# Two hybrid decoder layers: separate PSUM banks for even and odd blocks of a norm, later column sums, mLSTM heads ahead of MoBA, and the residual behind the convolutions

## The chip, the core and the metric

One core of a Trainium2 chip runs the whole program. TensorE (PE) does the matrix products, VectorE (DVE), ScalarE (ACT) and GpSimd (POOL) work on tiles of 128 partitions in the on-chip memory, and SyncE (SP) issues the loads from HBM. Products land in PSUM, eight banks of 128 x 512 float32, which DVE and ACT read. The metric is the device time of one execution in microseconds; the median of the runs counts.

## What is computed

A trunk of two layers on 256 tokens of width 1024, all in float32. Each layer has three sublayers, each with a modulation from a conditioning vector and a layer norm behind it:

```
def reference(x, c, ...):
    for l in range(DEPTH):
        mod = (silu(c) @ ada_w[l] + ada_b[l]).reshape(b_, 3, 3, D_MODEL)
        y = swiglu(modulate(x, mod[:, 0, 0], mod[:, 0, 1]), ffn_w13[l, 0], ffn_w2[l, 0])
        x = layer_norm(ALPHA * x + 0.5 * (1 + mod[:, 0, 2]) * y, ln_g[l, 0], ln_b[l, 0])
        y = token_mixer(modulate(x, mod[:, 1, 0], mod[:, 1, 1]), w_in[l], w_out[l], ...)
        x = layer_norm(ALPHA * x + (1 + mod[:, 1, 2]) * y, ln_g[l, 1], ln_b[l, 1])
        y = swiglu(modulate(x, mod[:, 2, 0], mod[:, 2, 1]), ffn_w13[l, 1], ffn_w2[l, 1])
        x = layer_norm(ALPHA * x + 0.5 * (1 + mod[:, 2, 2]) * y, ln_g[l, 2], ln_b[l, 2])
```

The token mixer projects the input once (`w_in`) and gives the columns to three groups of heads of width 64: six heads of a gated delta rule (GDN) over chunks of 64 tokens, with a causal convolution and SiLU ahead; four heads of MoBA, which for 256 tokens is causal softmax attention; six mLSTM heads, also with a convolution ahead, whose output is multiplied with a sigmoid of a gate projection, normed per head and scaled. The three outputs stand side by side (`mix`) and go through `w_out`.

## The kernel before

The program has six phases in a row, FFN, mixer, FFN for each layer, with a boundary (layer norm, modulation, start of the next phase) between any two.

**Products.** Each float32 weight comes by DMA into a tile `raw` and is split: ACT copies it to a rounded `hi` (L101), DVE subtracts to `lo` (L104). Each product is three matmuls (`mm3`, L109 to L111), with hi and lo of both sides. The splits run all through the kernel, so ACT and DVE have weight splits between whatever else they do.

**Order.** SP's order is that of the code. For PE, DVE and ACT a scheduler sorts the instructions of each phase; inside a boundary, from the norm to the first lines of the next phase, the order is that of the code too. `tc.issue_after` holds an instruction behind another.

**Boundary.** `Norm` reads the finished PSUM rows in two token halves t = 0, 1: `gate` multiplies with the gate row (L320), `add` adds the residual `xa` (L325), `square` and `stats` make the statistics, `scale` normalises (L354). `turn(t, q)` transposes four 128 x 128 blocks k of a half into one PSUM bank (L440); `mod` applies scale and shift per block into `xm`, even k on ACT (L450), odd k on DVE (L448); `high` (L454) and `low` (L459) split the outcome into `xh` and `xl`, which the first product of the next phase takes (`nx["product"]`). Some of the adaptation columns are summed here (`late`, L225, matmuls of one column with `ones`).

**Adaptation.** `ada_block` computes one of nine blocks of `silu(c) @ ada_w` in four background items (`bg`) within the FFN phases: DVE accumulates `adacc` from loads `araw` (L260). `fin` then sums over partitions on PE, as columns (L225) or, for a gate block, as broadcast rows (L233). For blocks in `late` the boundary calls `fin`; for all others the fourth item does.

**Mixer.** `gt` and `zs` are copied from the first product. `gdn_sink` runs convolution and SiLU on each projected block (`conv_silu`: ACT L731, DVE L733 three times, ACT L735) and squares keys and queries on POOL (`sq`, L771), whose head sums PE takes (L773). The generator `gdn` prepares decays (`g`, `ge` L889, `kg` L887, `eG` L900) and, after solving the chunk systems, runs the recurrence over four chunks (state `S`, L1093 to L1137). Behind it comes the residual of the sublayer (`residual`, two loads `gb` and four DVE operations), the convolution of mLSTM's q and k (`mqk`), and then generators whose steps are called in turn: `mlstm` (gates, decay weights `MB` and `Wx`; scores and weighted sums of six heads, L1199 to L1210; the tail `hc`, `mva`, `mix`, L1220 to L1239) and `moba` (scores L1254 to L1261, transposed probabilities L1274, output L1285). `mlstm_gate` (L832) applies the sigmoid to `so`, 128 x 768. `mix_T` transposes columns of `mix` (L301) and splits them for the output product (L303, L304).

**Output rows.** `out_rows` goes through `w_out` in four pairs of row blocks k; the last two pairs are held back and multiplied in the boundary. Blocks 0 to 2 are GDN's, 3 and 4 MoBA's, 5 to 7 mLSTM's.

## Time and profile before

| | |
|---|---|
| runs | 1236.38, 1231.99, 1237.64 us; median 1236.38 |
| profiled execution | 1231.17 us, span 1229.5 |
| PE busy | 1160.3 us, 94% |
| DVE, ACT, POOL busy | 894.8 (73%), 578.4 (47%), 107.2 us (9%) |

The span in order: FFN to 231 us, boundary, mixer 255 to 416, held products and boundary to 440, FFN to 636, boundary, and the second layer: FFN to 836, boundary, mixer 855 to 1009, boundary, FFN to 1210, final norm. PE idles where a row of the waits names it, and the clock column (PEclk) says at what share of its full clock it ran. A wait in brackets in the timeline, `[0.94 <-ACT xh L454]`, is the idle time just before the instruction and what ended it.

### The profile page before, as it was taken

How to read it: one execution, taken by the hardware profiler on the slowest of the kernel's cores; microseconds unless marked ns; L12 is line 12 of the kernel's file. 1: busy time of each engine (PE TensorE's matmuls, PEld its weight loads, DVE VectorE, ACT ScalarE, POOL GpSimd, SP SyncE). 2: the span in 40 equal slices, each digit the busy share in tenths (PEclk: the TensorE clock that was granted, in tenths of full speed). 3: DMA queues.
4: the chain of work that ended last, by engine and by line, in shares of the span. 5: the costliest groups of instructions: out<-in, count | busy, mean ns of one | idle time of the engine just before them, and what ended most of it. 6: DMA issues, size and time to landing. Idle time of an engine off the chain costs nothing.

```text
span 1229.5 us, 21037 instructions
## 1 busy us (share of the span) xinstructions
PE 1160.3 (94%) x8584; PEld 1051.4 (86%) x8584; DVE 894.8 (73%) x1423; ACT 578.4 (47%) x934; POOL 107.2 (9%) x174
## 2 busy tenths in 40 slices
PE   6899999988999799999999999999999979999996
PEld 4899988788997678999778999888898867999984
DVE  7889977677665679888578877776884766756655
ACT  3355443366573355544335554435755625544431
POOL 1000000012511200000000000001332120000001
PEclk9899999989998899999999999998999989999998
DMA  9999797363342159987638977671643431765650
GB/s 307 343 320 369 277 410 292 119 184 127 122 148 85 35 191 354 325 313 291 237 140 283 365 260 280 252 275 51 209 125 126 161 113 33 258 224 178 234 206 34
DMA packets 171522, 265.99 MB, mean 216 GB/s; under 512 B 5407, under 2 KB 136987, under 8 KB 171425
## 3 DMA queue, kind: packets, MB, share of 16 engines
q1 hardware_dynamic: 170368, 262.32, 62.1%
q10 hardware_dynamic: 1056, 2.32, 0.5%
q8 instruction: 67, 1.10, 0.4%
q14 instruction: 31, 0.25, 0.1%
HBM read 263.56 MB, written 1.06 MB: 215 GB/s over the span
## 4 chain that ended last, share of the span: by engine, by line
PE 77%; DVE 8%; DMA 5%; ACT 4%; POOL 3%; issue 2%; SPq 0%; DVEq 0%; ACTq 0%; POOLq 0%
PE pg L110 14%; PE pg L109 14%; PE pg L111 14%; PE pacc L109 9%; PE pacc L111 8%; PE pacc L110 8%; DMA raw<-in_ffn_w_dram 3%; DVE lo L104 2%; PE pg L225 1%; POOL xt L976 1%; POOL X L978 1%; ACT xm L450 1%; PE pg L233 1%; ACT hi L101 1%; DMA araw<-in_ada_w_dram 1%
## 5 line engine op out<-in xcount | busy, mean ns | idle before, releaser
L104 DVE TENSOR_TENSOR lo<-raw,hi 128x1024 fp32r<-128x1024 f32 (+3 forms) x332 | 396.4, 1200 | 163.4 <-PE pg L111 73.0
L101 ACT ACTIVATE hi<-raw 128x1024 fp32r<-128x1024 f32 (+4 forms) x352 | 353.9, 1027 | 294.8 <-DMA raw<-in_ffn_w_dram 113.3
L109 PE MATMUL pg<-xh,hi 128*128 128x256 f32 x1568 | 447.6, 287 | 5.4 <-ACT xh L604 2.7
L110 PE MATMUL pg<-xl,hi 128*128 128x256 f32 x1568 | 447.6, 286 | 1.5 <-DVE xl L607 1.5
L111 PE MATMUL pg<-xh,lo 128*128 128x256 f32 x1568 | 445.7, 285 | 0.0
L109 PEld LDWEIGHTS pg<-xh,hi 128*128 128x128 f32 x1568 | 301.9, 193 | 8.1 <-ACT xh L604 3.4
L110 PEld LDWEIGHTS pg<-xl,hi 128*128 128x128 f32 x1568 | 303.7, 194 | 3.4 <-DVE xl L607 2.0
L111 PEld LDWEIGHTS pg<-xh,lo 128*128 128x128 f32 x1568 | 303.2, 194 | 0.3
L260 DVE SCALAR_TENSOR_TENSOR adacc<-araw,sc__132,adacc 128x1024 f32<-128x1024 f32 x118 | 150.9, 1279 | 4.9 <-DMA araw<-in_ada_w_dram 4.1
L110 PE MATMUL pacc<-lo,hh 128*128 128x512 f32 x352 | 139.8, 397 | 1.6 <-DVE lo L104 1.5
L109 PE MATMUL pacc<-hi,hh 128*128 128x512 f32 x352 | 140.8, 400 | 0.0
L111 PE MATMUL pacc<-hi,hl 128*128 128x512 f32 x352 | 139.6, 396 | 0.0
L110 PEld LDWEIGHTS pacc<-lo,hh 128*128 128x128 f32 x352 | 66.3, 188 | 19.4 <-DVE lo L104 3.4
L109 PEld LDWEIGHTS pacc<-hi,hh 128*128 128x128 f32 x352 | 66.3, 188 | 16.4 <-issue 0.7
L111 PEld LDWEIGHTS pacc<-hi,hl 128*128 128x128 f32 x352 | 66.3, 188 | 15.9
L177 POOL TENSOR_TENSOR lsm<-lsm,mhalf 128x1 f32<-128x1 f32 x12 | 7.9, 660 | 701.1 <-DVE lsm L349 701.1
L632 ACT ACTIVATE sg<-pg 128x256 f32<-128x256 f32 x79 | 29.5, 375 | 81.2 <-PE pg L111 77.0
L639 ACT ACTIVATE hh<-h 128x256 fp32r<-128x256 f32 x82 | 33.8, 412 | 47.2 <-DVE h L634 46.8
L640 DVE TENSOR_TENSOR hl<-h,hh 128x256 fp32r<-128x256 f32 x82 | 34.4, 420 | 19.5 <-ACT hh L639 19.5
L109 PE MATMUL pacc<-hi,xh 128*128 128x512 f32 (+1 forms) x80 | 34.1, 427 | 10.2 <-ACT xh L454 10.2
L733 DVE SCALAR_TENSOR_TENSOR cy<-pg,cvc,cy 128x255 f32<-128x255 f32 (+2 forms) x90 | 40.1, 473 | 4.2 <-ACT cy L731 3.7
L339 ACT ACTIVATE lsq<-n,lsm 128x512 bf16<-128x512 f32 x24 | 17.3, 720 | 49.3 <-DVE lsm L328 31.5
(377 smaller groups left out, 1398.8 us busy)
## 6 DMA issues: line engine op xcount, KB each, us to landing
raw<-in_ffn_w_dram SPq DMA_DIRECT2D x118, 1024.0 KB, 5.7
araw<-in_ada_w_dram SPq DMA_DIRECT2D x64, 1024.0 KB, 8.6
raw<-in_w_in_dram SPq DMA_DIRECT2D x16, 1024.0 KB
araw<-in_ada_w_dram SPq DMA_DIRECT2D x16, 512.0 KB, 6.5
raw<-in_w_out_dram SPq DMA_DIRECT2D x8, 1024.0 KB, 4.8
raw<-in_ffn_w_dram SPq DMA_DIRECT2D x16, 448.0 KB, 6.1
raw<-in_ffn_w_dram SPq DMA_DIRECT2D x14, 512.0 KB, 4.5
raw<-in_w_in_dram SPq DMA_DIRECT2D x8, 792.0 KB, 6.7
```

Of the source, the lines that this page charges most:

```text
L101: state["hi"] = nc.scalar.activation(hi, v, AF.Copy)
L104: state["lo"] = nc.vector.tensor_tensor(lo[j], v[:, j * m:(j + 1) * m, :], hi[:, j * m:(j + 1) * m, :].bitcast(F32), op=ALU.subtract)
L109: nc.tensor.matmul(o, ah, bh, start=first, stop=False)
L110: nc.tensor.matmul(o, ah, bl, start=False, stop=False)
L111: nc.tensor.matmul(o, al, bh, start=False, stop=last)
L225: nc.tensor.matmul(pt[:, m:m + 1], acc[:, m * 128:(m + 1) * 128], ones[:, 0:1], start=True, stop=True)
L260: nc.vector.scalar_tensor_tensor(acc, raw[:, kk, :], sc_[:, k:k + 1], acc, op0=ALU.mult, op1=ALU.add)
L339: return nc.scalar.activation(sq[:, :c1 - c0], self.n[:, t, c0:c1], AF.Square, bias=self.cols(t, 6), accum_out=self.cols(t, 3 + h))
L632: nc.scalar.activation(sg, pa, AF.Silu)
L639: nc.scalar.activation(hh[:, f, :], h, AF.Copy)
L640: nc.vector.tensor_sub(hl[:, f, :], h, hh[:, f, :].bitcast(F32))
L733: nc.vector.scalar_tensor_tensor(y[:, s:], ps[:, :T - s], w(3 - s), y[:, s:], op0=ALU.mult, op1=ALU.add)
```

## The change

Each part in words, then the diff:

- `turn` takes two banks for four blocks: even k go to one, odd k to the other. For t = 1 the banks are two `acc1` ones and then two of the `g` ones.
- The late column sums stand behind `turn(1, 0)` and `turn(1, 1)` on PE, ahead of them before.
- For blocks that aren't late, `fin` is a fifth background item of its own.
- The copies `gt` and `gi` go from DVE to ACT, the squares `sq` from POOL to ACT.
- `residual` is called behind the mqk convolutions, and its operations are held behind the last SiLU.
- The gate becomes Exp of the negative on ACT, and on DVE plus one and RECIPROCAL, and it is called behind the first step of `ml`, ahead of the heads.
- mLSTM's remaining steps come before the remaining steps of MoBA; MoBA's columns (3, 4) of `mix` are transposed last and are the last pair in `out_rows`.

```diff
--- before.py
+++ after.py
@@ -258,13 +258,11 @@
                                 nc.vector.tensor_scalar(acc, raw[:, kk, :], sc_[:, k:k + 1], None, op0=ALU.mult)
                             else:
                                 nc.vector.scalar_tensor_tensor(acc, raw[:, kk, :], sc_[:, k:k + 1], acc, op0=ALU.mult, op1=ALU.add)
-                    if i == 3 and late is None:
-                        fin()()
-                    elif i == 3:
+                    if i == 3 and late is not None:
                         late.append(fin)
                 return run
 
-            return [chunk(i) for i in range(4)]
+            return [chunk(i) for i in range(4)] + ([lambda: fin()()] if late is None else [])
 
         bg = []
 
@@ -435,15 +433,17 @@
             pts, xms, left = {}, {}, []
 
             def turn(t, q):
-                pts[t, q] = v = (ps_acc(1) if t else ps_g()).rearrange("p (a b) -> p a b", a=4)
+
+                pts[t, q] = v = [(ps_acc(1) if t and not q else ps_g()) for _ in range(2)]
                 for k in range(4):
-                    nc.tensor.transpose(v[:, k, :], nr.n[:, t, (4 * q + k) * 128:(4 * q + k + 1) * 128], ident)
+                    nc.tensor.transpose(v[k % 2][:, k // 2 * 128:k // 2 * 128 + 128],
+                                        nr.n[:, t, (4 * q + k) * 128:(4 * q + k + 1) * 128], ident)
                 xms[t, q] = ap_.tile([128, 4, 128], F32, tag="xm", name="xm", bufs=2)
 
             def mod(t, *ks):
 
                 for k in ks:
-                    o, v = xms[t, k // 4][:, k % 4, :], pts[t, k // 4][:, k % 4, :]
+                    o, v = xms[t, k // 4][:, k % 4, :], pts[t, k // 4][k % 2][:, k % 4 // 2 * 128:k % 4 // 2 * 128 + 128]
                     if k % 2:
                         nc.vector.tensor_scalar(o, v, sp[:, k:k + 1], bp[:, k:k + 1], op0=ALU.mult, op1=ALU.add)
                     else:
@@ -489,11 +489,11 @@
             nr.scale(1, 0, 512)
             nr.scale(1, 512, 1024)
             ps = [nx["product"](0, xh, xl)]
+            turn(1, 0)
+            turn(1, 1)
             if late:
                 pt = ps_g()
                 left = [fin(pt[:, i * 8:i * 8 + 8]) for i, fin in enumerate(late)]
-            turn(1, 0)
-            turn(1, 1)
             mod(1, 0, 1, 2, 3)
             high(1, 0, 2), low(1, 0, 2)
             high(1, 2, 4), low(1, 2, 4)
@@ -744,7 +744,7 @@
             if l == 0:
                 late_constants()
             for t in range(2):
-                nc.vector.tensor_copy(gt[:, t, :], pz[t][:, 0:12])
+                nc.scalar.activation(gt[:, t, :], pz[t][:, 0:12], AF.Copy)
                 state["ln_act"] = nc.scalar.activation(zs[:, t, :], pz[t][:, 12:396], AF.Copy)
             state["ln_dve"] = state["lo"]
             state["region"].close()
@@ -768,7 +768,7 @@
                 conv_silu(ps, 0, 9, blk, dst)
                 if w < 2:
                     r = mp.tile([128, T], F32, tag="sq", name="sq")
-                    nc.gpsimd.tensor_mul(r, dst, dst)
+                    nc.scalar.activation(r, dst, AF.Square)
                     for ct in range(2):
                         nc.tensor.matmul(ss4[:, ct, 2 * p:2 * p + 2], r[:, ct * 128:(ct + 1) * 128], hs, start=True, stop=True)
 
@@ -786,12 +786,13 @@
                 nc.gpsimd.tensor_mul(z3, z3, gnrm[l].unsqueeze(1).to_broadcast([128, 6, 64]))
             for _ in gd:
                 pass
-            state["residual"]()
             mqk = mp.tile([128, 6, T], F32, tag="mqk", name="mqk")
 
             def mqk_sink(blk, ps):
                 conv_silu(ps, 72, 6, blk, mqk[:, blk, :])
             proj_T(2316, [(0, 1), (2, 3), (4, 5)], mqk_sink)
+            with tc.issue_after(state["silu"].ins):
+                state["residual"]()
             part.close()
             stage.enter_context(banks(f"psC{l}", (("mb", 2),)))
             state["after"] = state["silu"].ins
@@ -802,7 +803,7 @@
                 nc.gpsimd.memset(vc[:, :, :, 64:65], 1.0)
                 gi = mp.tile([128, 2, 12], F32, tag="gi", name="gi")
                 for t in range(2):
-                    nc.vector.tensor_copy(gi[:, t, :], pv[t][:, 384:396])
+                    nc.scalar.activation(gi[:, t, :], pv[t][:, 384:396], AF.Copy)
                     nc.scalar.activation(vc[:, t, :, 0:64], pv[t][:, 0:384].rearrange("p (h d) -> p h d", d=64), AF.Copy)
                 ml = mlstm(l, mp, mix, mqk, vc, gi)
                 next(ml)
@@ -828,17 +829,19 @@
                 state["so"] = so
 
             def mlstm_gate():
-                with tc.issue_after(state["exp"].ins):
-                    state["exp"] = nc.scalar.activation(state["so"], state["so"], AF.Sigmoid)
+
+                so = state["so"]
+                with tc.issue_after(state["after"]):
+                    nc.scalar.activation(so, so, AF.Exp, scale=-1.0)
+                nc.vector.tensor_scalar(so, so, 1.0, None, op0=ALU.add)
+                nc.vector.reciprocal(so, so)
             ml = mlstm_in()
             mo = moba_in()
             moba_v()
             mlstm_o()
             next(ml)
-            for _ in mo:
-                pass
+            mlstm_gate()
             next(ml)
-            mlstm_gate()
 
             def parts(name, *tags):
                 tiles = [(k0, k1, mp.tile([128, n, T], F32R, tag=tag, name=name)) for k0, k1, n, tag in tags]
@@ -849,11 +852,13 @@
                 return view
             mh = parts("mh", (0, 5, 6, "KQ"), (5, 8, 3, "kk"))
             mlo = parts("mlo", (0, 3, 3, "g1"), (3, 5, 3, "g2"), (5, 8, 3, "vv"))
-            mix_T(mix, mh, mlo, [(3, 5, 0, 2)], ps_mb)
             mix_T(mix, mh, mlo, [(0, 3, 0, 1), (0, 3, 1, 2)], ps_d)
             for _ in ml:
                 pass
+            for _ in mo:
+                pass
             mix_T(mix, mh, mlo, [(5, 7, 0, 2), (7, 8, 0, 2)], ps_d)
+            mix_T(mix, mh, mlo, [(3, 5, 0, 2)], ps_mb)
             stage.close()
             return lambda k, t: (mh(k, k + 1)[:, 0, t], mlo(k, k + 1)[:, 0, t])
 
@@ -1336,7 +1341,7 @@
                         tags = (("nl", 1024),), (("AT", 768), ("Y", 768)), (("mqk", 1536),), (("t6", 1536),)
                         return [mp.tile([128, n], F32R, tag=tag, name="nlo") for tag, n in tags[i]]
                     nx["low"] = low
-                    rest = end(*out_rows(lhs, w_out[l], [(3, 4), (0, 1), (2, 5), (6, 7)], nx))
+                    rest = end(*out_rows(lhs, w_out[l], [(0, 1), (2, 5), (6, 7), (3, 4)], nx))
             else:
                 with fstack if (l, s) == (0, 0) else tc.tile_pool(name=f"ff{l}{s}", bufs=1, reuse_waits="tile") as fp:
                     if (l, s) != (0, 0):
```

What the scheduler makes of it is shown at three places. Names are those of the tiles, and line numbers of the changed kernel are shifted by up to five. First PE at the first boundary, after the product of t = 0; `n` is the normed row, `adacc` the late accumulators. Before:

```order
L111 MATMUL pacc_2417<-hi,xl 128x396
L225 MATMUL pg<-ones,adacc 128x1 x16
L440 MATMUL pacc_2459<-ident,n 128x128 x4
L440 MATMUL pacc_2465<-ident,n 128x128 x4
L109 MATMUL pacc_2485<-hi,xh 128x396
```

Now:

```order
L111 MATMUL pacc_2419<-hi,xl 128x396
L439 MATMUL pacc_2444<-ident,n 128x128
L439 MATMUL pacc_2445<-ident,n 128x128
L439 MATMUL pacc_2444<-ident,n 128x128
L439 MATMUL pacc_2445<-ident,n 128x128
L439 MATMUL pg<-ident,n 128x128 x4
L225 MATMUL pg<-ones,adacc 128x1 x16
L109 MATMUL pacc_2489<-hi,xh 128x396
```

The transposes alternate between two banks, and the column sums moved from ahead of them to behind them, next to the first product of t = 1.

Second, DVE in the recurrence of the first mixer, around chunk 1; `S` is GDN's state, `un` the chunk's new values, `so` the gate, `mP` the weighted scores of an mLSTM head, `bnm` MoBA's maxima. Before:

```order
L1119 TENSOR_TENSOR S<-Sd,pgdn 64x3x64 x2
L1131 TENSOR_REDUCE ms<-oq 128x6
L1136 TENSOR_TENSOR mix<-pgdn,zs 128x384
L1254 TENSOR_REDUCE bnm<-pmb 128x1
L1256 TENSOR_SCALAR bnm<-bnm 128x2
L1255 TENSOR_REDUCE bnm<-pmb 128x1
L1132 TENSOR_SCALAR ms<-ms 128x6
L1096 TENSOR_TENSOR un<-U,pgdn 64x384
```

Now:

```order
L1124 TENSOR_TENSOR S<-Sd,pgdn 64x3x64 x2
L836 TENSOR_SCALAR so<-so 128x768
L1136 TENSOR_REDUCE ms<-oq 128x6
L1141 TENSOR_TENSOR mix<-pgdn,zs 128x384
L837 RECIPROCAL so<-so 128x768
L1137 TENSOR_SCALAR ms<-ms 128x6
L1208 SCALAR_TENSOR_TENSOR mP<-pg,MB 128x256
L1209 SCALAR_TENSOR_TENSOR mP<-pg,Wx 128x128
L1101 TENSOR_TENSOR un<-U,pgdn 64x384
```

The two gate operations and an mLSTM head stand where MoBA's maxima stood.

Third, DVE at the end of the first mixer, from the statistics of the second three mLSTM heads (`mva`) to the split of the transposed columns (`mlo`). Before:

```order
L104 TENSOR_TENSOR lo<-raw,hi 128x1024 x2
L1233 TENSOR_REDUCE mva<-hsq 128x6
L104 TENSOR_TENSOR lo<-raw,hi 128x1024
L104 TENSOR_TENSOR nlo<-raw,hi 128x1024
L1234 SCALAR_TENSOR_TENSOR mva<-mva,mrd 128x6
L104 TENSOR_TENSOR lo<-raw,hi 128x1024
L104 TENSOR_TENSOR nlo<-raw,hi 128x1024
L1235 TENSOR_TENSOR mva<-mva,mrd 128x6
L1236 TENSOR_SCALAR mva<-mva 128x6
L1238 TENSOR_TENSOR mva<-mva,mrd 128x6
L1239 TENSOR_TENSOR mix<-mix,mva 128x2x192
L304 TENSOR_TENSOR mlo<-pgdn,mh 128x512
```

Now:

```order
L1243 TENSOR_TENSOR mva<-mva,mrd 128x6
L1244 TENSOR_TENSOR mix<-mix,mva 128x2x192
L1259 TENSOR_REDUCE bnm<-pmb 128x1
L1260 TENSOR_REDUCE bnm<-pmb 128x1
L1261 TENSOR_SCALAR bnm<-bnm 128x2
L302 TENSOR_TENSOR mlo<-pgdn,mh 128x512
L1259 TENSOR_REDUCE bnm<-pmb 128x1
L1260 TENSOR_REDUCE bnm<-pmb 128x1
L302 TENSOR_TENSOR mlo<-pgdn,mh 128x256
L1261 TENSOR_SCALAR bnm<-bnm 128x2
L1288 RECIPROCAL bsm<-bsm 128x8
L1290 TENSOR_TENSOR mix<-pm,bsm 128x256 x2
```

MoBA's rows stand behind the mLSTM tail now, and no weight split stands between the steps of that tail.

## Rows read from the trace of the kernel before

**Rows 1.** The page: the span, and the busy time of each engine.

```profile
span 1229.5 us, 21037 instructions
PE 1160.3 (94%) x8584; PEld 1051.4 (86%) x8584; DVE 894.8 (73%) x1423; ACT 578.4 (47%) x934; POOL 107.2 (9%) x174
```

**Rows 2.** What PE waits for: who waits, for whom, us in total, times, longest.

```profile
PE pgdn L301 <- DVE mix L1239: 11.9, 2, 6.0
PE pacc L109 <- ACT xh L454: 10.2, 10, 1.4
PE pm L773 <- POOL sq L771: 5.6, 4, 1.9
...
PE pg L233 <- DVE adacc L260: 2.5, 1, 2.5
PE pgdn L894 <- DVE ge L889: 1.9, 1, 1.9
PE pmb L1274 <- ACT bP L1261: 1.5, 1, 1.5
...
PE pg L109 <- DVE sk L778: 1.5, 1, 1.5
...
PE pgdn L914 <- ACT eG L900: 1.2, 1, 1.2
```

**Rows 3.** Timeline of the first boundary, t = 1: start, us, instruction, idle before.

```profile
239.55 4.38 PE L225 MATMUL pg<-ones,adacc 128*128 128x1 f32 x32
...
244.92 0.46 ACT L450 ACTIVATE xm<-pacc,bp,sp 128x128 f32<-128x128 f32 x1 [5.81 <-PE pacc L440]
...
245.42 0.41 DVE L448 TENSOR_SCALAR xm<-pacc,sp,bp 128x128 f32<-128x128 f32 x1 [4.35 <-ACT xm L450]
...
246.68 0.70 PE L109 MATMUL pacc<-hi,xh 128*128 128x396 f32 x1 [0.94 <-ACT xh L454]
```

**Rows 4.** Stretches: width, busy PE, PEld, DVE, ACT, POOL, PEclk, DMA share, GB/s.

```profile
231.00:255.00 24.00, 21.91 (x113) 19.99 (x113) 13.32 (x39) 10.80 (x23) 2.67 (x7) 0.79 0.04 8
366.00:420.00 54.00, 45.06 (x271) 36.54 (x270) 33.17 (x78) 19.14 (x42) 10.54 (x10) 0.84 0.24 78
480.00:490.00 10.00, 7.54 (x39) 5.83 (x39) 8.07 (x11) 6.97 (x10) 0.96 (x1) 0.83 1.07 368
966.00:1014.00 48.00, 41.40 (x277) 33.84 (x278) 31.20 (x75) 17.43 (x37) 10.53 (x10) 0.93 0.35 119
```

**Rows 5.** Groups of POOL and ACT by shape (busy, mean ns); a DVE timeline row.

```profile
L771 POOL TENSOR_TENSOR sq<-kT 128x256 f32<-128x256 f32 x6 | 5.2, 869 | 7.9 <-ACT kT L735 5.0 <-PE pm L773 1.9 <-ACT KQ L735 0.8
...
L731 ACT ACTIVATE cy<-pg,cvc 128x256 f32<-128x256 f32 x30 | 13.1, 459 | 0.0
...
268.95 3.62 DVE L519 TENSOR_TENSOR xa<-xa,gb 128x1024 f32<-128x1024 f32 x2
```

**Rows 6.** Groups of DVE by shape: out<-in, count, busy, mean ns, idle before.

```profile
L354 DVE TENSOR_SCALAR n<-n,lsm 128x512 f32<-128x512 f32 x20 | 10.2, 551 | 3.5 <-POOL lsm L177 3.5
...
L1203 DVE SCALAR_TENSOR_TENSOR mP<-pg,MB 128x256 f32<-128x256 f32 x12 | 5.0, 418 | 5.6 <-PE pg L1201 5.6
...
L1131 DVE TENSOR_REDUCE ms<-oq 128x6 f32<-128x384 f32 x4 | 2.2, 554 | 1.5 <-ACT oq L1129 1.5
...
L1222 DVE RECIPROCAL mrd<-mrd 128x6 f32<-128x6 f32 x4 | 0.7, 181 | 0.0
...
L1236 DVE TENSOR_SCALAR mva<-mva 128x6 f32<-128x6 f32 x4 | 0.7, 172 | 0.1
...
L1283 DVE RECIPROCAL bsm<-bsm 128x8 f32<-128x8 f32 x2 | 0.4, 204 | 1.1 <-ACT bP L1261 1.1
...
L881 DVE RECIPROCAL be__2579<-be__2579 128x12 f32<-128x12 f32 x1 | 0.2, 228 | 0.0
...
L873 DVE TENSOR_SCALAR xa__2568<-xa__2568 128x12 f32<-128x12 f32 x1 | 0.2, 166 | 0.0
```

**Rows 7.** PE timeline in the recurrence: its six products with the state S.

```profile
370.97 0.87 PE L1093 MATMUL pgdn<-S,WT 128*64 128x128 f32 x6
```

## The prediction

> **What bounds the kernel now.** The page first: TensorE (PE) is busy 1160.3 of a span of 1229.5 us, every other engine 73% or less [rows 1]. So only what lets PE stand still, or run at its lower clock, can be won. The profiled execution took 1231.17 us, 1.7 us more than its span; the median of the three runs is 1236.38, 5.2 us above it. I make the sum against the profiled execution and put the result on the scale of the median.
>
> Second, the list of what PE waits for [rows 2]. Its idle time has a few places: the last mixer transposes wait for the mLSTM tail on VectorE (DVE), 11.9 us in two waits; the first products behind each norm wait for ScalarE (ACT), 10.2 us in ten; the head of the mixer waits for POOL squares, for `ge`, `eG` and `sk`; the adaLN gate block (0,8) waits 2.5 us once for its accumulator.
>
> Third, the stretches around these places, for the clock [rows 4]. Granted 0.79 in the first long boundary, 0.84 in the end of mixer 0, 0.93 in the end of mixer 1: behind a stop PE runs for a while at the 1.2 GHz level. A stop costs its length and then half of the busy time at that level.
>
> **The change part by part.**
>
> **Boundaries.** Before, the four transposes of a half share one bank; ACT and DVE take turns on it, which the timeline shows: ACT 244.92 to 245.38, then DVE from 245.42, which waited 4.35 us, for ACT at last [rows 3]. Four turns are 0.46 + 0.41 + 0.46 + 0.41 = 1.74 us and about 0.1 between them. With even blocks in ACT's bank and odd ones in DVE's, no wait orders them: 2 x 0.46 = 0.92 beside 2 x 0.41. That is 0.9 us off each half. Two of the four halves of a boundary have a PE wait behind them (ten waits, 10.2 us [rows 2], among them the 0.94 in [rows 3]). Ten times 0.9 would be 9; some of these waits, for t = 0 above all, have the gate, add and scale steps on DVE behind them as well, and a half is not released sooner if those are late. I take 0.7 each: -7. Where column sums are late (4.38 us of PE in [rows 3], at three of the five boundaries) they now stand behind the transposes of t = 1 and run while ACT and DVE modulate, which speaks for the full size there. Bounds: -3 (only these three lose their t = 1 wait) to -10.2 (all ten waits gone). I count no gain of clock: 0.79 over 24 us is 5.0 us of clock, but the stop behind the norm itself stays.
>
> **Mixer heads.** The squares go from POOL, 0.87 us each [rows 5], to ACT, where a 128x256 activation takes 0.46 [rows 5]; PE's four waits for them are 5.6 us. The copies `gt` and `gi` move to ACT; both are tens of columns. The residual (its two additions alone take DVE 3.62 us in the timeline [rows 5], two multiplications stand ahead of them) goes behind the mqk convolutions, so that `ge` and the convolutions come 6 us sooner on DVE. This is what PE's waits for `ge` (1.9), `eG` (1.2) and `sk` (1.5) stand behind [rows 2]. Together 10.2 us. What is late next: convolutions on DVE, which feed the same square, and ACT, which has the squares and copies on top of its activations but is busy for only 47% of the span. The residual's two loads on SP now stand three weight loads later in SP's queue, which brings these weights sooner; its own reader is the norm at the end of the mixer, over 100 us on. The residual's DVE work later on falls beside PE projections, so it costs nothing unless DVE lags the weight splits there. I take -7 of 10.2, bounds -1 (only the wait for `ge`, and half of it) and -10.2.
>
> **Adaptation blocks.** `fin` becomes a background item of its own. At (0,8) the gate rows on PE move behind 28 more matmuls (by the order); at 1160.3 / 8584 = 0.135 us each that is 3.8 us, more than the wait of 2.5 [rows 2]. The stretch 480 to 490 runs at 0.83 [rows 4]: 1.7 us of clock. Sum 4.2. Against it: the accumulator's buffer is freed later, so the following raw load starts later. I take -3, bounds 0 and -4.2. The other blocks had no wait worth a row.
>
> **The mLSTM gate.** Sigmoid becomes Exp on ACT, plus one, and a DVE RECIPROCAL of 128x768. The trace has no such wide one, but small ones [rows 6]: 128x6 in 181 ns, 128x8 in 204, 128x12 in 228, while other operations do not grow from 128x6 (172) to 128x12 (166). Between these, 6.0 (8 to 12) to 7.8 ns (6 to 12) per element; 768 elements at 7.1, between the two, with 0.13 us fixed, are 5.6 us. Bounds: 0.8 us, if it is like the scalar operation, 0.551 us for 512 elements; and 8.9 us by the steepest pair (6 to 8: 11.5 ns). I take 5.6, which is nearest to the rows of the same operation.
>
> The Trainium skill ("VectorE: DVE Perf Modes", section "First, the fixed hardware budget") says that Reciprocal runs as an iterative divide with a repeat count of 8; eight cycles of the 0.96 GHz of its section "Specifications" are 8.3 ns an element and, as an estimate, 6.4 us for 768. The rows' growth of 6.0 to 7.8 ns agrees roughly; by the page the tails would come out 1.6 us worse in the two layers.
>
> Where it stands decides its price. By the order it lies in DVE's queue inside the recurrence: behind it wait the next `ms`, the probabilities `mP` of a head and `un`, which PE needs for its next chunk. From the state S of chunk 1 DVE has: plus one 0.8, `ms` reduction 0.55, a `mix` product about as long, reciprocal 5.6, a small `ms` step 0.17, `mP` 0.7 (the 0.418 of [rows 6] and one half as wide), 8.4 us. PE has in that time its products with S, 0.87 for six [rows 7], and the scores of a head, estimated at 1.4 from the same pace: 2.3. So PE stops for about 6.0 us in layer 0; in layer 1, where the plus one comes earlier, 5.4. Each stop is as long as the old tail wait (longest 6.0 [rows 2]) and is followed by lower clock as that was. In layer 1 the stretch of the tail lost 2.3 us to clock (next paragraph) around its one long stop; I take 2.3 for each.
>
> **Mixer tails.** Before: 366 to 420 has 54.0 - 45.06 = 8.9 us idle and 0.16 x 54 = 8.6 us of clock; 966 to 1014 has 6.6 idle and 0.07 x 48 = 3.4 of clock [rows 4]. Some low clock falls into the idle time itself, where it costs nothing; I take off 1.2 and 1.1, which leaves 7.4 and 2.3. Together 25.2. After: heads now run ahead of MoBA, and between the mLSTM tail's small steps DVE has no weight splits any more, so that the two waits for `mix` (11.9) go. In their place come the reciprocal's stop and its clock (6.0 + 2.3 and 5.4 + 2.3), and what stands at the end now: the probabilities of MoBA (PE waited 1.5 for `bP` once [rows 2]; I take that), the copies of their transposes and the last `mix` ahead of its transposes (1 each), the last head's `mP` behind a power on POOL (1), 4.5 us a layer, with half of a stop's clock, 1.2; and 0.4 a layer of small idle time as before. That is 14.4 + 13.8 = 28.2. So the tails cost +3. With a reciprocal of 0.8 us the stops shrink to 1.2 and 0.6 and lose no clock: 14.0, a gain of -11.2. With 8.9 us both grow by 3.3: +9.6.
>
> **The sum.** -7 - 7 - 3 + 3 = -14: 1217 on the profiled scale, **1222** on that of the median.
>
> **The rivals.** *The reciprocal is cheap.* Then the old waits for `mix` go and little comes for them: -7 - 7 - 3 - 11.2 = -28.2, 1208. For it: a 128x512 scalar operation takes 0.551. Against: the growth from 6 to 12 elements, which no other operation shows.
>
> *The boundaries do not do what they say.* The banks are free, but the chain of gate, add, statistics and scale on DVE ends last, and PE waits just as long: without the -7 the time is 1229. For it: DVE has 13.3 of 24 us busy in that boundary [rows 4] and the additions go through it one by one. Against: ACT and DVE wait for each other at each turn in [rows 3], and PE's wait names `xh` just behind them.
>
> *The clock stays down: slower.* The reciprocal's stop lies amid a stage of small matmuls. If PE stays at 1.2 GHz from there to the end of the mixer, in both layers, every microsecond of PE's work done there takes one more. In 366 to 420 PE has 45.06 busy, about 17 of it low already (0.16 x 54 x 2), so 28 at full clock; in 966 to 1014 41.4 less 6.7, so 35. All of it doubled is +63, half of it +31. This rival decides from +20 (14 and the 0.5% that follows), a third of it; at half it gives 1236.4 - 14 + 31 = 1253. For it: 0.84 at the end of mixer 0. Against: 0.93 in layer 1 behind a stop just as long (6.0), so the clock came back in between.
>
> **How the numbers follow.** Forecast 0.57, cheap reciprocal 0.15, boundaries without gain 0.18, low clock 0.10. About 0.5% (6.2 us) is what a measurement of this kernel can tell from no change. The forecast's own ends (tails +9.6 with heads -1 and the rest small) reach no change: 0.47 faster, 0.10 same. Boundaries without gain stand at 1229, on the border: 0.08 faster, 0.10 same. So faster 0.70, same 0.20, slower 0.10. The range goes from 1205, below the cheap reciprocal, to 1238, above the boundaries without gain and the forecast with a steep reciprocal; the low clock is left out.
>
> **What would show it.** The RECIPROCAL of 128x768 with its own duration, 5 to 6 us, and a PE wait of about 6 for `un` or `mP` behind it; at the boundaries ACT and DVE modulating at once and PE's `xh` waits down from 10.2 to some 3 us; no PE wait for squares in the heads; the wait for `mix` of the mLSTM (11.9) gone; the wait at (0,8) gone. Wrong would be: a reciprocal that lies beside PE's work, a new wait in the boundary that is as long as the old, or a clock below 0.8 over a whole mixer.

## The result, and the profile after

The changed kernel takes 1240.96 us (median of 10), the kernel before 1233.33: a ratio of 1.0059, 95% interval 1.0046 to 1.0072. It is slower by 7 us where 14 us less were forecast, and lies above the range. (The forecast's 1222 stood on the 1236.38 of the first three runs of the kernel before; from 1233.33 the same forecast would be 1219.) The profiled execution has a span of 1239.1 against 1229.5 [rows 1].

The page of the changed kernel, span and busy times:

```profile
span 1239.1 us, 21043 instructions
PE 1173.9 (95%) x8584; PEld 1067.0 (86%) x8584; DVE 904.2 (73%) x1419; ACT 576.8 (47%) x952; POOL 100.7 (8%) x162
```

PE is busy 13.6 us longer with the same 8584 matmuls, so its idle time fell (69.2 to 65.2 us) while the span grew: in sum a matter of the clock. What PE waits for now (in all, times, longest), to be held against [rows 2]:

```profile
PE pg L109 <- DVE cy L733: 8.0, 3, 4.9
PE pg L1212 <- DVE mP L1209: 6.3, 3, 4.7
...
PE pm L773 <- ACT sq L771: 3.4, 2, 1.7
...
PE pm L1285 <- ACT bPT L1281: 1.9, 3, 0.6
...
PE pacc L109 <- ACT xh L454: 1.3, 2, 0.6
...
PE pmb L299 <- DVE mix L1290: 1.0, 2, 0.5
...
PE pgdn L299 <- DVE mix L1244: 0.8, 1, 0.8
```

The old waits are gone or small: the last `mix` of the mLSTM from 11.9 to 0.8 (and 1.0 for MoBA's, which is the last one now), `xh` from 10.2 to 1.3, squares from 5.6 to 3.4. Large now are `cy`, 8.0, and `mP`, 6.3, both about 1 before:

```profile
PE pg L109 <- DVE cy L733: 1.1, 2, 0.9
PE pg L1207 <- DVE mP L1204: 1.0, 2, 0.8
```

Both traces were cut at the same products (at the first, 400th, 440th ... matmul of line L109), so that each stretch holds nearly the same work. A mixer is cut in two: its head with decays and convolutions, and its tail with the recurrence, the mLSTM heads, MoBA and the last transposes. Width of each in us:

| stretch | before | after | difference |
|---|---|---|---|
| first FFN, to the held rows | 182.59 | 186.50 | +3.9 |
| end of the first FFN | 30.92 | 35.63 | +4.7 |
| five boundaries | 126.19 | 115.23 | -11.0 |
| heads and convolutions, both mixers | 191.41 | 195.46 | +4.1 |
| tails, both mixers | 138.25 | 149.34 | +11.1 |
| FFN behind mixer 0 | 184.54 | 181.21 | -3.3 |
| the other two FFNs | | | 0.0 |

The differences add up to the 9.6 us of the span within 0.2. The end of the first FFN and the tails of both mixers in the views of stretches, first before (the columns are those of [rows 4]):

```profile
202.37:233.29 30.92, 29.74 (x130) 23.01 (x128) 24.24 (x33) 9.30 (x14) 0.55 (x1) 1.00 0.73 246
...
350.27:422.92 72.65, 63.71 (x471) 52.79 (x470) 44.64 (x104) 31.02 (x72) 11.62 (x13) 0.88 0.27 87
...
953.76:1019.36 65.60, 59.00 (x462) 48.95 (x462) 44.32 (x104) 29.76 (x68) 11.98 (x12) 0.95 0.37 126
```

and after:

```profile
206.48:242.11 35.63, 32.27 (x130) 24.69 (x128) 26.20 (x36) 9.69 (x17) 0.55 (x1) 0.90 0.72 243
...
358.60:434.66 76.06, 67.88 (x476) 55.88 (x475) 50.69 (x106) 30.61 (x72) 13.35 (x14) 0.87 0.25 83
...
958.28:1031.56 73.28, 69.73 (x476) 56.41 (x476) 51.15 (x111) 29.53 (x70) 10.79 (x13) 0.86 0.31 100
```

Idle time of the tails (width less busy PE) fell from 15.5 to 11.7 us. Width times what the clock lacks of 1 rose from 8.7 + 3.3 to 9.9 + 10.3. The tail of layer 1, with only 3.55 us idle, ran at 0.86.

Each new loss has its rows. **The end of the first FFN**, chain that ended last, start and us:

```profile
217.34 1.30 DVE adacc L260
...
218.65 0.37 SPq L82
...
219.12 7.11 DMA raw<-in_ffn_w_dram
...
226.33 1.06 ACT hi L101
```

SP's own rows there, before and then after:

```profile
204.08 1.14 SPq L82 DMA_DIRECT2D araw<-in_ada_w_dram  x2
209.29 0.37 SPq L82 DMA_DIRECT2D raw<-in_ffn_w_dram  x1
```

```profile
208.19 10.83 SPq L82 DMA_DIRECT2D araw<-in_ada_w_dram  x3
219.12 0.54 SPq L82 DMA_DIRECT2D raw<-in_ffn_w_dram  x1
```

In the changed kernel three adaptation loads stand at SP until 219.02; the last of them could go when VectorE's accumulation at 217.34 had freed a buffer. The last weight load of the phase stands behind it and is issued at 219.12. Before, two adaptation loads stood ahead of it and it was out at 209.29. With fin an item of its own, one more item was left when the phase ended, and it was a load.

**The mixer head of layer 1**, SP's rows, then one of VectorE:

```profile
874.62 0.34 SPq L510 DMA_DIRECT2D gb<-in_ln_g_dram  x1
875.01 0.42 SPq L511 DMA_DIRECT2D gb<-in_ln_b_dram  x1
886.27 1.55 SPq L82 DMA_DIRECT2D raw<-in_w_in_dram  x2
```

```profile
878.44 2.36 DVE L518 TENSOR_TENSOR xa<-n,gb 128x1024 f32<-128x1024 f32 x2 [3.89 <-DMA gb<-in_ln_g_dram]
```

The residual's operations were called behind the mqk convolutions and meant to be held behind the last SiLU, but on VectorE they still stand behind the sixth of the 45 convolution operations of the layer (before, behind the second): the scheduler let them through. Their loads went out later than before (861.67 there), so VectorE waited 3.89 us with convolutions behind it. `gb` takes one of the four `raw` buffers, and SP issued no weight load from 875.4 to 886.27, when the last operation that reads `gb` had just ended (886.25). SP's waits for these operations, over the whole program, before and then after:

```profile
SPq L82 <- DVE xa L519: 5.7, 2, 4.5
```

```profile
SPq L82 <- DVE xa L519: 18.3, 4, 6.4
```

This is the PE wait of 4.9 us for `cy`; the first experiment below takes it away.

**The reciprocal**: its group (count, busy, mean ns), its place in layer 0, and the PE row behind it:

```profile
L837 DVE RECIPROCAL so<-so 128x768 f32<-128x768 f32 x2 | 9.9, 4944 | 0.0
```

```profile
380.53 4.94 DVE L837 RECIPROCAL so<-so 128x768 f32<-128x768 f32 x1
...
386.06 0.69 PE L1212 MATMUL pg<-vc,mP 128*128 128x65 f32 x2 [4.73 <-DVE mP L1209]
```

In layer 1 PE had other work and hardly stopped, yet the clock fell there too. Stretches of layer 1, with the reciprocal from 977.25 to 982.20:

```profile
974.00:978.00 4.00, 3.63 (x38) 3.02 (x38) 3.94 (x12) 0.77 (x2) 0.72 (x2) 0.99 0.60 246
978.00:982.00 4.00, 4.00 (x17) 3.23 (x16) 4.00 (x1) 0.28 (x1) 0.29 (x1) 0.50 0.00 0
982.00:986.00 4.00, 3.69 (x22) 3.06 (x22) 3.25 (x11) 0.49 (x2) 0.86 (x1) 0.50 0.01 2
986.00:990.00 4.00, 4.00 (x27) 3.46 (x23) 3.49 (x12) 0.52 (x1) 1.89 (x4) 0.50 0.01 2
990.00:994.00 4.00, 4.00 (x16) 3.47 (x16) 1.69 (x5) 0.28 (x1) 1.04 (x1) 0.50 0.02 4
```

PE is "busy" 4.00 of 4.00 us, and at the 1.2 GHz level. Ahead of it stood 0.37 us of idle time and small matmuls of the recurrence and the heads. The clock fell at about 978, less than a microsecond behind the start of the RECIPROCAL at 977.25, so the 4.9 us that this one held VectorE cannot have brought the fall in layer 1; whether it made it last longer is not shown by this trace.

**The boundaries** did what was meant; timeline of the first one, to be held against [rows 3]:

```profile
248.81 0.81 ACT L450 ACTIVATE xm<-pacc,bp,sp 128x128 f32<-128x128 f32 x2 [2.14 <-PE pacc L439]
248.93 0.73 DVE L448 TENSOR_SCALAR xm<-pacc,sp,bp 128x128 f32<-128x128 f32 x2 [0.30 <-PE pacc L439]
249.17 5.26 PE L225 MATMUL pg<-ones,adacc 128*128 128x1 f32 x32
```

ScalarE and VectorE modulate side by side, under the column sums. The two boundaries behind the mixers have no late column sums and shortened by 2.2 and 2.5 us, so there the banks alone do it; the other three, with both parts, gave 2.3, 2.8 and 1.1. PE's waits for `n` ahead of the transposes grew from 0.7 to 3.0 us in all.

### The profile page after: what moved, and what is told of

It reads as the page before. It is cut to its first block, busy times and chain, and to the rows that moved or that the text cites. A ratio compares the mean times of both kernels' runs of the same rounds, so it can differ in the third digit from the quotient of the medians.

```text
span 1239.1 us, 21043 instructions
## 1 busy us (share of the span) xinstructions
PE 1173.9 (95%) x8584; PEld 1067.0 (86%) x8584; DVE 904.2 (73%) x1419; ACT 576.8 (47%) x952; POOL 100.7 (8%) x162
## 4 chain that ended last, share of the span: by engine, by line
PE 74%; DVE 10%; DMA 6%; ACT 4%; issue 3%; POOL 3%; SPq 0%; DVEq 0%; ACTq 0%; POOLq 0%
PE pg L109 13%; PE pg L110 13%; PE pg L111 13%; PE pacc L109 8%; PE pacc L110 8%; PE pacc L111 8%; DMA raw<-in_ffn_w_dram 3%; DVE lo L104 3%; PE pg L225 2%; POOL X L983 1%; ACT hi L101 1%; DMA raw<-in_w_in_dram 1%; PE pg L233 1%; POOL xt L981 1%; DVE so L837 1%
## 5 line engine op out<-in xcount | busy, mean ns | idle before, releaser
L109 PE MATMUL pg<-xh,hi 128*128 128x256 f32 x1568 | 448.5, 288 | 12.9 <-DVE cy L733 7.8
L109 PEld LDWEIGHTS pg<-xh,hi 128*128 128x128 f32 x1568 | 303.6, 195 | 15.3 <-DVE cy L733 8.0
L109 PE MATMUL pacc<-hi,hh 128*128 128x512 f32 x352 | 142.0, 404 | 2.5 <-ACT hi L101 2.5
L109 PEld LDWEIGHTS pacc<-hi,hh 128*128 128x128 f32 x352 | 66.8, 190 | 19.5 <-ACT hi L101 3.0
L634 DVE TENSOR_TENSOR h<-sg,pg 128x256 f32<-128x256 f32 x79 | 32.6, 415 | 9.8 <-ACT sg L632 6.0
```

The lines of the kernel that those rows point to most:

```text
L109: nc.tensor.matmul(o, ah, bh, start=first, stop=False)
L634: nc.vector.tensor_mul(h, sg, pb)
```

## The experiments

Ratios are to the kernel before, with 95% intervals; 0.001 is 1.2 us. A caution that holds for all: the scheduler sorts anew for each edit, so some of the order elsewhere in the mixer moves as well.

**Residual at its old place**

```diff
+            state["residual"]()
             mqk = mp.tile([128, 6, T], F32, tag="mqk", name="mqk")
...
-            with tc.issue_after(state["silu"].ins):
-                state["residual"]()
```

> The changed kernel with the residual called at its old place, ahead of the mqk convolutions; all else as changed. Theory 1 (the residual loads now stand behind weight loads in SP's queue, hold two of the four raw buffers late, and DVE waits for them at the head of its queue while convolutions stand behind): the PE waits of 2.9 and 4.9 us for cy in the two mixer heads go, the SP gap of 10.9 us in the second mixer head goes, and the time is 4 to 8 us below the changed kernel, 1233 to 1237. Theory 2 (these waits come from ACT, which has the squares and copies now): the waits stay, and the time is 1239 to 1243.

1.0159 (1.0145 to 1.0174): 12 us slower than the changed kernel. The waits for `cy` went, as theory 1 said, but waits for `ge` of 2.6 and 3.7 us and for squares (9.1 us in seven) took their place, and the mean clock fell from 0.960 to 0.951. Both theories missed the time, which went the other way. Moving the residual is a gain in this kernel, though it brings the wait for `cy`.

**No reciprocal**

```diff
-                nc.vector.reciprocal(so, so)
```

> The changed kernel without the two RECIPROCALs of 128x768, so that the gate is 1 + exp(-x) instead of its inverse; all else as changed. Theory 1 (the reciprocal holds DVE for 4.9 us, PE runs dry or thin behind it, and the clock falls for it): the PE wait of 4.7 us in mixer 0 goes and the 13.7 and 17.1 us at 1.2 GHz in the two mixers shrink to 3 to 7 each; 11 to 16 us faster than the changed kernel, 1225 to 1230. Theory 2 (the clock falls because the mLSTM heads and the recurrence run without MoBA beside them): only the wait goes, 3 to 5 us faster, 1236 to 1238, and both stretches stay over 10 us.

1.0013 (0.9990 to 1.0035), 5.7 us below the changed kernel, mean clock 0.965. That is between the two theories: more than the stop, less than all of the lower clock. The execution that was profiled took 1241.8 us, 9 above the median of its twelve. The wait of 4.7 us is gone in it and the tail of layer 1 runs at 0.95, but mixer 0 has two stretches at 1.2 GHz of 17.1 and 23.9 us, more than the changed kernel's 13.7. A piece of each:

```profile
339.00:355.00 16.00, 16.00 (x199) 15.37 (x200) 3.31 (x8) 4.02 (x9) 2.00 (x4) 0.50 0.31 109
391.00:413.00 22.00, 21.29 (x88) 18.04 (x89) 12.35 (x37) 5.09 (x18) 5.18 (x6) 0.50 0.15 48
```

So a long stretch of low clock needs no RECIPROCAL; that leaving it out gives 6 us is read from the medians alone.

**fin back in the fourth item**

```diff
-                    if i == 3 and late is not None:
+                    if i == 3 and late is None:
+                        fin()()
+                    elif i == 3:
                         late.append(fin)
...
-            return [chunk(i) for i in range(4)] + ([lambda: fin()()] if late is None else [])
+            return [chunk(i) for i in range(4)]
```

> The changed kernel with fin back inside the fourth item of each adaptation block. Theory 1 (items of their own push the last adaptation loads of the first FFN ahead of its last weight load in SP's queue, 4.7 us at the end of that phase and 4.1 us in its first 120 us, while the wait at block (0,8) is saved): the first FFN is 5 to 9 us shorter, the wait of 2.5 us and its low clock come back in the FFN behind mixer 0 (+4); 1 to 5 us faster, 1236 to 1240. Theory 2 (the first FFN differs from execution to execution): it stays as long as in the changed kernel, and the time is 4 us longer, 1245.

1.0069 (1.0053 to 1.0085). The first FFN is back at 212.3 us (before 213.5, after 222.1), which settles that its loss comes from fin. The time did not move: in this profile the tails take 155.3 us where they took 149.3, at 0.78 and 0.84. The first part of theory 1 held (9.9 us, a little more than it said, and the wait at (0,8) is back with 2.2 us), its total didn't; in this trace what was regained went to the clock of the mixers' tails.

**MoBA ahead of the heads again**

```diff
-            mlstm_gate()
+            for _ in mo:
+                pass
             next(ml)
+            mlstm_gate()
...
+            mix_T(mix, mh, mlo, [(3, 5, 0, 2)], ps_mb)
             mix_T(mix, mh, mlo, [(0, 3, 0, 1), (0, 3, 1, 2)], ps_d)
...
-                    rest = end(*out_rows(lhs, w_out[l], [(0, 1), (2, 5), (6, 7), (3, 4)], nx))
+                    rest = end(*out_rows(lhs, w_out[l], [(3, 4), (0, 1), (2, 5), (6, 7)], nx))
```

> The changed kernel with MoBA ahead of the mLSTM heads again, its columns transposed first and its rows of w_out taken first; the gate remains Exp, plus one and RECIPROCAL, called behind the heads' first steps as before. Theory 1 (the reciprocal is what lowers the clock): low clock of over 10 us in the mixers remains, and the old waits for the last mix of the mLSTM (11.9 us) come back: 5 to 12 us slower, 1246 to 1253. Theory 2 (the order is what lowers the clock): the low stretches of 13.7 and 17.1 us go, the old waits come back: 0 to 8 us faster, 1233 to 1241.

1.0082 (1.0053 to 1.0111): with the reciprocal in place the order makes 3 us, within the intervals. The waits for the last `mix` are back (12.8 us), as both theories said, and that for `mP` of 4.7 is gone. The run doesn't tell the theories apart.

**The boundary part alone, on the kernel before** (`mod` reads from the two banks accordingly)

```diff
-                pts[t, q] = v = (ps_acc(1) if t else ps_g()).rearrange("p (a b) -> p a b", a=4)
+                pts[t, q] = v = [(ps_acc(1) if t and not q else ps_g()) for _ in range(2)]
...
+            turn(1, 0)
+            turn(1, 1)
             if late:
...
-            turn(1, 0)
-            turn(1, 1)
```

> The kernel before with the boundary part of the change alone: even and odd blocks in banks of their own, late column sums behind the transposes. Theory 1 (the five boundaries gain what the trace of the changed kernel shows there, 2.3, 2.2, 2.8, 1.1 and 2.5 us): 9 to 12 us faster than before, 1221 to 1225. Theory 2 (the clock gives the gain back in the stages behind): 1228 to 1234.

1.0066 (1.0046 to 1.0085): *slower* by 8 us. The boundaries gained 9.3 us in this trace, and the mixers lost 17, all of it in their heads: 6.5 us more idle time there, the rest lower clock (0.93 in both, from 1.00 and 0.98). The longest new wait of PE:

```profile
PE pgdn L895 <- DVE ge L890: 7.4, 2, 3.7
```

Before it was 1.9 in one layer. Both theories failed, the first by the sign.

**Boundary and residual, on the kernel before** (on the run above)

```diff
-            state["residual"]()
             mqk = mp.tile([128, 6, T], F32, tag="mqk", name="mqk")
...
+            with tc.issue_after(state["silu"].ins):
+                state["residual"]()
```

> The kernel before with two parts of the change: the boundary part and the residual behind the mqk convolutions. Theory 1 (the boundary alone lost its gain to a wait of 3.7 us for ge in each mixer head, behind the residual on VectorE, and the low clock after it; with the residual out of the way the gain stays): 10 to 16 us below the boundary part alone, 1226 to 1232, no wait for ge over 2 us. Theory 2 (the mixer head is late anyway): 1238 to 1243.

1.0006 (0.9991 to 1.0021), 7 us below the boundary alone. No wait for `ge` is in the list any more (waits for `kg` and squares of up to 2.6 remain). The time lies between the theories. The trace doesn't bear out theory 1 as the cause: with the waits for `ge` gone, the heads are 3.7 us shorter than in the run above and still 13.9 us longer than before, 3.9 of it idle time and the rest lower clock (0.97 and 0.92). What lowers the clock there, no run shows.

**Sigmoid at the new place**

```diff
-                    nc.scalar.activation(so, so, AF.Exp, scale=-1.0)
-                nc.vector.tensor_scalar(so, so, 1.0, None, op0=ALU.add)
-                nc.vector.reciprocal(so, so)
+                    nc.scalar.activation(so, so, AF.Sigmoid)
```

> The changed kernel with the gate as one Sigmoid on ScalarE, at the new place ahead of the heads. Theory 1 (RECIPROCAL on VectorE is what the gate costs): like the run without RECIPROCAL, 1229 to 1234, mean clock about 0.966, no PE wait of over 2 us for mP behind the recurrence. Theory 2 (the gate's new place is what costs, since ScalarE now loads tables there for Sigmoid and back): 1236 to 1242.

1.0002 (0.9984 to 1.0019), mean clock 0.966: theory 1. The gate's new form costs 7 us. Sigmoid at the new place is no slower than the run without RECIPROCAL (1.0013), so nothing is seen of the tables of theory 2; the new place by itself, with all else as before, was not run.

**The gate alone, on the kernel before**

```diff
+                so = state["so"]
...
-                    state["exp"] = nc.scalar.activation(state["so"], state["so"], AF.Sigmoid)
+                    state["exp"] = nc.scalar.activation(so, so, AF.Exp, scale=-1.0)
+                nc.vector.tensor_scalar(so, so, 1.0, None, op0=ALU.add)
+                nc.vector.reciprocal(so, so)
```

> The kernel before with the gate alone changed: Exp on ScalarE, plus one and RECIPROCAL of 128x768 on VectorE, called at the old place; MoBA ahead of the heads. Theory 1 (4.9 us of VectorE cost 4 to 5 us of PE each and lower clock): 1238 to 1245. Theory 2 (it costs only with the new order, in which nothing else is there for PE): 1231 to 1235.

1.0134 (1.0110 to 1.0158): 16 us slower, above the range of theory 1. The old order, too, pays for it: in the trace the tails are 14.9 us longer than before, 7.4 of it idle time.

**Sigmoid, and fin an item of its own for block (0,8) only** (below: the fast version)

```diff
                     if i == 3 and late is not None:
                         late.append(fin)
+                    elif i == 3 and (l, blk) != (0, 8):
+                        fin()()
...
-            return [chunk(i) for i in range(4)] + ([lambda: fin()()] if late is None else [])
+            return [chunk(i) for i in range(4)] + ([lambda: fin()()] if (l, blk) == (0, 8) else [])
```

> The changed kernel with Sigmoid on ScalarE and with fin an item of its own for block (0,8) alone, so that the first FFN has its old order. Theory 1 (the first FFN gets its 8.8 us back and the reciprocal's price is gone): 1220 to 1226, below the kernel before. Theory 2 (what the first FFN gets back is lost to the clock in the mixers, as with fin in its old form, where 5 to 9 us came back there): 1229 to 1234.

0.9907 (0.9883 to 0.9932), 1222.8 us: theory 1. Beside the run with Sigmoid alone (1.0002), the other blocks' fin cost 12 us here.

**The same with the reciprocal** (only the edit of fin)

> The changed kernel with fin an item of its own for block (0,8) alone; the gate with RECIPROCAL as changed. Theory 1 (fin's items of the other blocks cost the first FFN 9 to 11 us whatever the gate is): 1229 to 1233. Theory 2 (with RECIPROCAL the mixers' clock eats what the first FFN gets back, as with fin all in its old form): 1237 to 1242, mean clock under 0.960.

1.0008 (0.9984 to 1.0032), mean clock 0.959: 6 us below the changed kernel, 12 above the fast version. In the views of the tails, this run first, then the fast version:

```profile
349.10:426.69 77.59, 71.05 (x477) 58.21 (x475) 51.45 (x107) 30.75 (x72) 12.54 (x15) 0.80 0.25 82
954.54:1026.59 72.05, 64.94 (x461) 52.87 (x460) 48.68 (x107) 28.82 (x70) 12.06 (x12) 0.88 0.30 98
```

```profile
352.31:423.55 71.24, 65.11 (x477) 53.44 (x475) 45.49 (x105) 33.18 (x74) 12.88 (x15) 0.88 0.27 89
945.18:1013.39 68.21, 62.77 (x475) 50.85 (x475) 45.95 (x110) 32.09 (x73) 11.13 (x12) 0.92 0.33 108
```

Idle time differs by 2.1 us (13.7 and 11.6), the clock by 0.08 and 0.04: in this pair of traces the RECIPROCAL costs more by the clock than by stops. The time lies between the two theories.

**The reciprocal in six pieces, one behind each head** (on the run before this)

```diff
-                nc.vector.reciprocal(so, so)
...
+                last = nc.vector.scalar_tensor_tensor(Pm[:, 256:384], sc[:, 256:384], 0.125, Wx[:, h, :], op0=ALU.mult, op1=ALU.mult)
+                s6 = state["so"][:, :, h * 64:h * 64 + 64]
+                with tc.issue_after(last.ins):
+                    nc.vector.reciprocal(s6, s6)
```

> As the run with fin an own item for (0,8) alone and RECIPROCAL (1235.7), but the RECIPROCAL in six pieces of 128x128, each held behind the weighted scores of its head on VectorE; same VectorE time in all. Theory 1 (one operation of 4.9 us that holds everything behind it thins out PE's work and lowers the clock): 6 to 11 us faster, 1225 to 1230, mean clock 0.965 or more. Theory 2 (the VectorE time itself is what is missing): within 3 us, 1233 to 1239.

0.9966 (0.9948 to 0.9985): 5 us of the 12 come back, mean clock 0.963, at more VectorE time, not the same (six pieces of 0.941 us are 5.6). It lies between the theories: a part of the price is that one operation holds the queue. What the rest is was not told apart; the trace, at 1.2 GHz for 13.7 and 17.1 us in the tails, still has the low stretches.

**Residual at its old place, in the fast version** (the edit of the first experiment)

> The fastest version so far (changed kernel, Sigmoid on ScalarE, fin an own item for (0,8) alone; 1222.8) with the residual at its old place. Theory 1 (moving the residual is what lets the mixer head take up the shorter boundary, since the decay spread no longer stands behind it on VectorE): 8 to 12 us slower, 1230 to 1235, with PE waits for ge of 2.5 to 3.7 us in both heads. Theory 2 (the 11 us of the earlier run came from the mixers' clock behind RECIPROCAL): 1220 to 1226.

0.9943 (0.9916 to 0.9970): 4 us slower, with intervals that overlap. Between the two. The waits for `ge` are back as theory 1 said (2.5 in both heads, and 8.7 for squares), and those for `cy` are gone.

**One bank again, in the fast version** (the edit of the boundary part alone, the other way round)

> The fastest version so far with the four blocks of a boundary half in one bank again and the late column sums ahead of the transposes. Theory 1 (the boundaries' gain holds where the mixer head isn't behind): 8 to 11 us slower, 1231 to 1234, the waits for xh at the boundaries back at 10 us. Theory 2 (the mixer heads wait for VectorE, so that the two boundaries ahead of mixers bring nothing, the three ahead of FFNs keep theirs): 5 to 7 us slower, 1228 to 1230.

1.0048 (1.0024 to 1.0073): 17 us slower, more than either theory. The waits for `xh` are back at 10.2, and the boundaries took 11.0 us more in this trace, the mixers 3.8. This execution took 1234.7 us, 6.6 below the median; where the rest goes isn't seen, but the mean clock of all twelve is 0.963 against 0.967.

**Old order of MoBA and heads, in the fast version** (the edits of the fourth experiment, with the Sigmoid)

> The fastest version so far with MoBA ahead of the mLSTM heads, its columns transposed first and its rows of w_out first, and the Sigmoid at its old place. Theory 1 (the new order saves the waits for the last mix, 11.9 us, and gives back 4 to 6 in other waits and clock): 4 to 8 us slower, 1227 to 1231. Theory 2 (the new order lowers the clock as much as it saves): within 3 us, 1220 to 1226.

0.9862 (0.9836 to 0.9889), 1218.3 us, the fastest of all: the new order costs 5.5 us here (the intervals just touch), against both theories. The two waits for the last `mix` are back, 6.0 each; but the tails run at 0.92 and 0.95 and are 5.0 us shorter in all:

```profile
351.11:418.19 67.08, 60.49 (x477) 50.60 (x475) 45.10 (x105) 32.07 (x73) 13.28 (x15) 0.92 0.28 94
948.12:1015.46 67.34, 60.75 (x475) 50.45 (x475) 45.24 (x109) 30.94 (x71) 11.55 (x12) 0.95 0.35 116
```

The profiled execution took 1224.8 us, 6.4 above the median, and its heads are 5.7 us longer than the fast version's, so the gain of the medians can't be read from it.

**Squares and copies on their old engines, in the fast version** (the copy `gi` likewise)

```diff
-                nc.scalar.activation(gt[:, t, :], pz[t][:, 0:12], AF.Copy)
+                nc.vector.tensor_copy(gt[:, t, :], pz[t][:, 0:12])
...
-                    nc.scalar.activation(r, dst, AF.Square)
+                    nc.gpsimd.tensor_mul(r, dst, dst)
```

> The version with Sigmoid and fin an own item for (0,8) alone (1222.8), with the squares on GpSimd and the copies gt and gi on VectorE again. Theory 1 (PE's waits for squares go from 1.6 to 1.4 to 1.9 each and come twice as often): 2 to 5 us slower, 1225 to 1228. Theory 2 (the head waits for cy and the residual's rows instead, whichever engine squares): within 2 us.

0.9911 (0.9890 to 0.9933) against 0.9907: no difference, theory 2. PE waits 7.7 us for squares from POOL in place of 3.3 from ScalarE, and 5.0 for `cy` in place of 8.4.

**Residual later still, in the fastest version**

```diff
-            with tc.issue_after(state["silu"].ins):
-                state["residual"]()
...
             ml = mlstm_in()
+            state["residual"]()
```

> The fastest version (Sigmoid, fin an own item for (0,8) alone, old order of MoBA and heads; 1218.3) with the residual called later still, behind the first step of the mLSTM part. Theory 1 (the waits of 3.4 and 5.0 us for cy in the mixer heads come from the residual's loads, for which VectorE waits at the head of its queue): both waits under 1.5 us, 4 to 8 us faster, 1210 to 1215. Theory 2 (they come from convolutions and splits themselves): within 3 us.

0.9930 (0.9906 to 0.9955): 8 us slower, against both theories. The waits for `cy` fell from 8.7 to 3.2 us in all, the longest from 4.8 to 1.6, so most of them come from the residual's loads, as theory 1 says. But the heads with the convolutions, 80 products into each mixer 12.8 us ahead of the run above, were 0.7 behind it at their end. The two profiled executions take the same time (1224.8 and 1224.4), so where the medians lose 8 us isn't seen. Taking the wait away in this manner did not pay.

## Why the prediction was wrong

Three terms failed, by the stretches of the two traces: mixer heads (-7 forecast, +4.1 measured), adaptation blocks (-3, and +8.6 in the first FFN beside -3.3) and tails (+3, +11.1).

**Boundaries, -7.** The mechanism was right and the size nearly: -11.0 in the trace, a little beyond the bound of -10.2; idle time fell by 6.6, waits for `xh` from 10.2 to 1.3. What doesn't hold is that such a term can be added to the end as it is. Alone it made the kernel 8 us slower, since the mixer heads lost more than the boundaries gave. The wait for `ge` behind the residual on VectorE is a part of that; the larger part is low clock in the heads, which stayed with this wait gone and whose cause is open. Together with the moved residual the pair cost nothing, and in the fast version the boundary part is worth 17.

**Mixer heads, -7.** Measured +4.1. The waits named in [rows 2] for squares and `ge` did shrink, but the squares were worth nothing (0.9911 against 0.9907). The step that failed was that the moved residual "costs nothing". It did not go behind the convolutions on VectorE, which the forecast took for granted. I named the queue that its loads pass, not that VectorE waits for these loads at the head of its own queue, nor that they sit in a buffer of the weight loads. The price was waits for `cy` of 8.0 us in place of 1.1. Beside them the heads ran at a lower clock, 0.96 and 0.95, before 1.00 and 0.98. Even so the move is worth 12 us in the changed kernel, and 4, with overlapping intervals, in the fast version.

**Adaptation blocks, -3.** Right for (0,8): the wait went and the FFN behind mixer 0 shortened by 3.3. Wrong was "The other blocks had no wait worth a row": a wait absent before is no bound on one that a moved load makes. The first FFN lost 8.6 us (with fin back, none of it). With fin back for all blocks but (0,8), 6 and 12 us came back in two pairs of runs.

**The gate.** The duration was well bounded, 4.94 us against 5.6; per element it is (4944 - 941) / 640 = 6.25 ns from the two widths, near the 6.0 between 8 and 12 elements [rows 6]. The Trainium skill ("VectorE: DVE Perf Modes", section "First, the fixed hardware budget") with its repeat count of 8 had given an estimate of 6.4 us; the measurement decides for less. The stop in layer 0 was 4.7 of 6.0. In layer 1 it hardly was there (5.4 forecast): PE had heads and chunk products to do. Yet the tail of layer 1 grew most, by the clock. Over the runs the gate's new form cost 6 to 16 us in four pairs (the runs without RECIPROCAL, with Sigmoid, with Sigmoid in the fast version, and the gate alone), where the forecast's two stops with their clock are 16.0.

**Tails, +3.** Measured +11.1. The waits for `mix` went as said. The term that was mis-sized is the clock: 2.3 us a stop, taken from stops, where low clock came without a stop. In the forecast's 28.2 for the tails, 21.2 are idle time and 7.0 clock; the trace has 11.7 and 20.2. Over both mixers, heads and tails, idle time went from 27.6 to 26.3 us and width times missing clock from 13.9 to 29.0; that is nearly all of the 15.2 us that the mixers lost.

**The rivals.** "The clock stays down" was given 0.10 and was the right kind: same place, both layers, though the stop that it names as the cause was there in layer 0 alone. It asked for +20 to decide; the mixers' clock gave some 15 and the first FFN 8.6, against boundaries that gave 11. Its reason against, that layer 1 kept 0.93 behind a stop of 6.0, was no reason: in the changed kernel the clock fell in layer 1 with no stop ahead of it. A cheap reciprocal is refuted; that the boundaries change nothing by themselves is refuted, too.

What stays open: the parts do not add. The new order of MoBA and heads makes -3 us with the reciprocal (within the intervals) and +5.5 without, fin of the other blocks +6 or +12, the boundary part +8 alone, 0 together with the residual and -17 in the fast version. Block (0,8) alone makes 7 us between the run with all of fin back (1.0069) and the one with fin for (0,8) alone (1.0008), where the FFN behind mixer 0 differs by 2.2. Each edit also re-sorts the mixer, and runs of one kernel differ by their clock (0.951 to 0.968 in twelve of the one with fin for (0,8) alone and the reciprocal); a single trace shows one of them, as the run without RECIPROCAL does with 41 us at 1.2 GHz in mixer 0. How much of a difference is the sort and how much the clock was not told apart, nor what makes the clock fall in the mixers.

## What to carry to other kernels

Before a load is moved, list what shares its queue and its buffers, and who waits for it at the head of an in-order engine: two edits that took waits of 2 to 3 us away brought losses of 4 to 5 elsewhere. On an engine that is 94% busy, read the granted clock by stage beside the idle time, in more than one execution, and do not price low clock by the stops alone. Undo the parts of a bundle one by one, in the fastest version as well as in the first: here the bundle was 7 us slower and three of its parts left out made it 17 us faster than before.

## What was not expected of the hardware

PE fell to 1.2 GHz from about 978 to 995 us with 0.37 us of idle time ahead of it, while it was busy 19.32 of the 20 us from 974 to 994. In the run without RECIPROCAL it was at 1.2 GHz from 339 to 355 us with no idle time in these 16 us. A RECIPROCAL of 128x768 took 4.94 us where a scalar operation of the same shape took 0.55 (`so` plus one); in pieces of 128x128 it took 0.94 each.
